# Gate/up of an encoder trunk: all engines in written order, evictions ahead of conversions, silu and products one product later

## The chip, the cores and the metric

The kernel runs on one core of a Trainium2 chip. The metric is the time of one execution in microseconds of device time (us). Before the change it is 2461.02 us, the median of 3 runs (2459.26 to 2463.18).

A core has five instruction streams that run beside each other and meet through semaphores: TensorE (PE in the profile, its weight loads PEld), VectorE (DVE), ScalarE (ACT), GpSimd (POOL) and SyncE (SP), which here issues the transfers between the chip's memory and the on-chip buffers. Matrix products land in eight banks of an accumulation memory (PSUM), from where VectorE or ScalarE has to take them. Each stream executes its instructions in the order in which the program holds them.

## The reference

Two layers of an encoder on 1024 tokens of width 1024. A layer has an attention half and a feed-forward half; the change touches the second, of which the core is

```
h = rms_norm(x, g_ffn[l]) * (1 + sc_f) + sh_f
gate, up = split_cols(h @ w_gu[l], (FFN_HIDDEN, FFN_HIDDEN))
x = x + gt_f * ((jax.nn.silu(gate) * up) @ w_down[l])
```

with `FFN_HIDDEN` = 2816. The vectors `sc_f`, `sh_f`, `gt_f` and three more for the attention half come from `mod = silu(c) @ w_mod[l] + b_mod[l]`, a product of one row with a 1024 x 6144 matrix per layer (the modulation).

## The kernel before

**Products in parts.** Each float32 operand is split into a high and a low part (`split_to`, line 205: ScalarE casts the high part, VectorE or GpSimd subtracts it from the source to get the low one), and `mm3` (line 197) multiplies in three matmuls. The matrix products of gate, up and down are done by a Strassen-Winograd scheme: a 2 x 2 block product in seven products instead of eight, with sums before and after. `PRODUCTS` (line 213) names the seven for gate/up in their order: number, the operand block of `h` it uses, and a bank a, b or c. Products 1, 6, 7 and 4 accumulate in bank a; between them a copy is taken out of the bank. So TensorE may not start product 6 before the copy after product 1 is taken, nor 7 before the copy "12" after 6, nor 3 (bank c) before the copy "22" after 5, nor 4 before the copy "x" after 7. One product is 4 x 3 = 12 matmuls of 128 x 128 by 128 x 512.

**Gate/up.** The 2816 columns of gate and of up are 11 pairs of column blocks. The loop runs over q = 0 to 21: even q is a gate block, odd q the up block of the same pair b = q // 2. For q below `EARLY` = 7 the first two products (1 and 2) are issued ahead of the loop, so the loop has five left for them and seven for the others. Operands on the weight side are made by a generator, `gu_parts` (line 1840): per q it loads the raw weights (`gu_raw`, names `wr`), makes four sums on VectorE (`ws`) and yields the converted parts (`wpt`). `ahead` holds up to 8 of them: `ahead.get()` (line 269) first fills the list to 8 and then takes one, and `ahead.fill()` after each product adds the next. The raw weights of odd q lie in buffers that before held blocks 2 and 3 of the activations (`x_tile`), and come free when their last split is done.

**After a product** (`gu_product`, line 1849): `take` copies a bank out on ScalarE, `add` adds a bank to an earlier copy on VectorE, `done` applies silu (ScalarE) for gate, or multiplies by up (GpSimd or VectorE). The result of a pair is two tiles `sg`, e and o, each of two halves. Two sets of these tiles take turns, so pair b + 2 overwrites pair b. They, too, lie in buffers of the activations.

**Down's operands** (`g_steps`, line 1900): a pair's four result blocks are stored (`gpd<-sg`), combined on VectorE by four subtractions (`sg<-sg`), and the combinations are stored as well. This is a list of 13 steps, of which one runs behind each product of the following pair (`g_step`); the stores come in steps 3, 9, 11 and 12, the subtractions in 8, 9 and 10. `gu_start` (line 1929) finishes what is left of the older pair when a new pair starts.

**Modulation** (`mod_stream`, line 353): in layer 0, from q = 7 on, each product is followed by one step of the next layer's modulation: a load of 128 x 512 weights (`wmt`) and one multiply-add on VectorE (`acc`), with two load buffers. In layer 1 nothing is left of it.

**The opening.** Ahead of the loop, `t2_part`, `t3_part` and `t4_part` (lines 1948 to 1976) make the remaining blocks of `h`: sums on VectorE in place (`xb`), then the splits `ht3`, `h22` and `ht4`, of which VectorE's halves are `ht3l`, `h22l` and `ht4l`.

**What sets the order.** Instructions are given to a scheduler, which may move them within an engine as long as data and buffers allow. `pin` (line 92) switches that off for chosen engines: each instruction is then bound to the one before it. In this loop, SyncE is pinned from the start (line 2003), ScalarE from the last q on (line 2008). Everything else is ordered by the scheduler.

Of the kernel before, what the change touches and what calls it, by code (L numbers as in the profile page):

```python
# [13 lines left out]
AF = mybir.ActivationFunctionType  # L14
ALU = mybir.AluOpType
# [8 lines left out]
H = 512  # L24
# [61 lines left out]
def trunk(ctx: ExitStack, tc, A, C, out):  # L86
# [266 lines left out]
    def mod_stream(psp, shared, until):  # L353


        pl, tag, bufs, width = shared
        acc = None
        while todo and todo[0] < until:
            l, g = todo[0]
            first = going["step"]  # L360
            if first == 0:
                going["acc"] = cp.tile([P, 1024], F32, name="acc", tag="acc")
            acc = going["acc"]
            halves = [(k, c0) for k in range(first, KC) for c0 in range(0, 1024, width)]
            loads = {}

            def load(i):
                k, c0 = halves[i]
                st = loads[i] = pl.tile([P, width], F32, name="wmt", tag=tag, bufs=bufs)
                g0 = g * 1024 + c0  # L370
                sp.dma_start(st, A["w_mod"][l, k * P : (k + 1) * P, g0 : g0 + width])

            if halves:
                load(0)
                yield
            for i, (k, c0) in enumerate(halves):
                if i + 1 < len(halves):
                    load(i + 1)
                mod_add(k, acc[:, c0 : c0 + width], loads.pop(i))
                yield  # L380
            going["step"] = KC
            mod_parts(slice(0, width), shared)
            while going["step"]:
                yield
                yield
                yield
                mod_flush(psp)
            yield
# [422 lines left out]
    for l in range(2):  # L811
# [1033 lines left out]
                raws = after or gu_raw(1)  # L1845

        sg, quads = {}, {}

        def gu_product(q, p, a):
            num, b, bank = p  # L1850
# [18 lines left out]
            def done(dst, src, eng=dve):  # L1869
                if up:  # L1870
                    eng.tensor_tensor(out=dst, in0=dst, in1=src, op=ALU.mult)
                else:
                    act.activation(dst, src, AF.Silu)

            if num == 1:
                take("11")
            elif num == 2:
                add("11")
                if e is not None:
                    done(e[:, lo], t["11"], pool)  # L1880
            elif num == 6:
                take("12", None if up else e[:, hi])
            elif num == 5:
                take("22", None if up else o[:, hi])
            elif num == 7:
                take("x")
                t22 = t["22"]
                pool.tensor_tensor(out=t22, in0=t22, in1=t["x"], op=ALU.add)
                done(o[:, hi], t["22"], pool)
            elif num == 3:  # L1890
                add("12")
                done(e[:, hi], t["12"], pool)
            else:
                done(o[:, lo], ps)
                if up:
                    steps.append(g_steps(q // 2, e, o))

        steps = []

        def g_steps(b, e, o):  # L1900


            b11, b12, b21, b22 = (t[:, i * H : (i + 1) * H] for t in (e, o) for i in range(2))

# [12 lines left out]

        def g_step():
            if steps:
# [80 lines left out]
        for part in (t3_part, t4_part):  # L2000
            for q in range(1, 4):
                part(q, *bs[q])
        pin([sp], True)
        for q in range(NF):
            if q % 2 == 0:
                gu_start(q // 2)
            if q == NF - 1:
                pin([act], True)
            if q < EARLY:
                up = q % 2  # L2010
                e = sg[q // 2][0][:, 0:H]
                if up:
                    pool.tensor_tensor(out=e, in0=e, in1=quads[q]["11"], op=ALU.mult)
# [339 lines left out]
```

## Time and profile before

| | |
|---|---|
| median of 3 runs | 2461.02 us (2459.26 to 2463.18) |
| the profiled execution | 2460.37 us, its span 2458.6 us |
| granted TensorE clock, mean | 0.991 |
| TensorE busy | 2390.3 us, 97% of the span |
| VectorE busy | 1821.8 us, 74% |
| ScalarE busy | 1224.9 us, 50% |
| GpSimd busy | 764.3 us, 31% |
| loop of gate/up, layer 0 | about 640 to 1044 us |
| loop of gate/up, layer 1 | about 1843 to 2227 us |

The span reaches from the first instruction to the last one. "PE ps_w" in the profile is a matmul of gate/up, "ps_d" one of down, "wpt" a converted part of a weight, "sg" a result tile, "u" a copy that was taken out of a bank, "gpd" the stored operands of down, "acc" the modulation's sum. All helpers record through line 49, so groups and rows are told apart by the tile names. A row of a timeline has start, duration, engine, line, operation, output and inputs, the count if several of a kind follow each other, and in brackets the idle time just before and what ended it.

### The profile page before, as it was taken

Reading aid. Unit: us, or ns where it says so; the run is one execution under the profiler, and the core shown is the slowest. Engines: PE = TensorE matmul, PEld = TensorE weight load, DVE = VectorE, ACT = ScalarE, POOL = GpSimd, SP = SyncE. Lnnn points to the kernel's source line nnn. Section 1 sums busy time; section 2 is a strip of 40 time slices with the busy share of each in tenths; the row PEclk is TensorE's granted clock in tenths of the full one; section 3 lists DMA queues with packets and bytes.
Section 4 is the critical chain, followed back from the end, with each engine's and each line's share of the span. In section 5 each row is a group of like instructions: output and inputs, shape, how many; then the busy total and the mean of one; then the engine's idle time right before and its main releaser. Section 6 shows DMA issues by size and latency. Waiting matters only on the chain.

```text
span 2458.6 us, 34285 instructions
## 1 busy us (share of the span) xinstructions
PE 2390.3 (97%) x12005; PEld 1992.7 (81%) x12005; DVE 1821.8 (74%) x2966; ACT 1224.9 (50%) x2306; POOL 764.3 (31%) x769
## 2 busy tenths in 40 slices
PE   8999999999999999999999999999999999999998
PEld 5787899878788877788887789987887888888886
DVE  5757999877967878587677679999698555446865
ACT  3422888954543333344544148888454333333443
POOL 1520444620244444300036114465005434430001
PEclk9999999999999999999999999999999999999999
DMA  8468205245345454496433851151624332229743
GB/s 287 147 177 287 54 14 146 57 151 167 95 142 173 158 168 140 154 287 201 129 116 106 259 195 27 41 152 44 210 90 141 125 115 95 99 102 283 215 134 110
DMA packets 285206, 356.04 MB, mean 145 GB/s; under 512 B 32997, under 2 KB 201533, under 8 KB 285033
## 3 DMA queue, kind: packets, MB, share of 16 engines
q1 hardware_dynamic: 277816, 341.12, 44.6%
q10 hardware_dynamic: 6912, 12.59, 1.6%
q8 instruction: 95, 1.56, 0.3%
q14 instruction: 79, 0.64, 0.1%
q0 software_dynamic: 304, 0.14, 0.0%
HBM read 269.62 MB, written 86.69 MB: 145 GB/s over the span
## 4 chain that ended last, share of the span: by engine, by line
PE 71%; DVE 11%; DMA 6%; issue 5%; ACT 4%; POOL 2%; SPq 1%; ACTq 0%; POOLq 0%; DVEq 0%
PE ps_w L49 30%; PE ps_d L49 10%; PE ps_o L49 7%; PE pv L49 6%; PE ps_ab L49 5%; PE T L49 4%; PE sC L49 3%; DVE wpt L49 2%; DMA wmt<-in_w_mod_dram 2%; PE ps_c L49 1%; ACT pr L49 1%; DMA zt<-skA 1%; PE sA L49 1%; DMA zAd<-zt 1%; DMA w<-in_w_down_dram 1%
## 5 line engine op out<-in xcount | busy, mean ns | idle before, releaser
L49 PE MATMUL ps_d<-wpt 128*128 128x512 f32 x1848 | 425.3, 390 | 2.0 <-DVE wpt L49 0.7
L49 PEld LDWEIGHTS ps_d<-wpt 128*128 128x128 f32 x1848 | 345.4, 188 | 77.2 <-DVE wpt L49 3.1
L49 POOL TENSOR_SCALAR pr<-pr,rs 128x1024 f32<-128x1024 f32 (+4 forms) x252 | 207.6, 826 | 308.5 <-DVE rs L49 290.7
L49 POOL TENSOR_TENSOR sg<-sg,u 128x512 f32<-128x512 f32 x86 | 124.2, 1445 | 360.9 <-ACT sg L49 228.0
L49 PE MATMUL pv<-pt,vs 128*128 128x256 f32 x1216 | 202.5, 297 | 8.0 <-DVE rs L49 2.3
L49 DVE TENSOR_TENSOR pt<-T,pt 128x512 fp32r<-128x512 f32 x304 | 199.4, 680 | 11.4 <-ACT pt L49 9.9
L49 ACT CAST pt<-T 128x512 fp32r<-128x512 f32 x304 | 170.2, 586 | 44.5 <-PE T L49 42.8
L49 PE MATMUL T<-identr,pr 128*128 128x128 f32 x1288 | 187.6, 273 | 2.2 <-ACT rb L49 1.0
L49 ACT COPY u<-ps_w 128x512 f32<-128x512 f32 x128 | 75.2, 587 | 215.1 <-PE ps_w L49 215.1
L49 PEld LDWEIGHTS pv<-pt,vs 128*128 128x128 f32 x1216 | 161.7, 190 | 23.2 <-DVE y L49 7.6
L49 DVE SCALAR_TENSOR_TENSOR acc<-wmt,condT,acc 128x512 f32<-128x512 f32 (+1 forms) x98 | 115.0, 1183 | 84.5 <-DMA wmt<-in_w_mod_dram 84.2
L49 DVE TENSOR_TENSOR wpt<-w,wpt 128x512 fp32r<-128x512 f32 x154 | 111.2, 722 | 84.0 <-ACT wpt L49 83.9
L49 PEld LDWEIGHTS T<-identr,pr 128*128 128x128 f32 x1288 | 153.1, 141 | 21.9 <-issue 3.2
L49 POOL TENSOR_TENSOR wpt<-ws,wpt 128x512 fp32r<-128x512 f32 x80 | 112.3, 1405 | 181.5 <-ACT wpt L49 139.3
L49 ACT CAST wpt<-w 128x512 fp32r<-128x512 f32 x154 | 95.5, 620 | 134.2 <-PE ps_d L49 127.9
L49 ACT CAST wpt<-ws 128x512 fp32r<-128x512 f32 x176 | 107.8, 622 | 56.4 <-issue 22.4
L49 ACT CAST wpt<-graw 128x512 fp32r<-128x512 f32 x154 | 95.0, 617 | 74.6 <-DMA graw<-gpd 65.2
L49 DVE TENSOR_TENSOR wpt<-ws,wpt 128x512 fp32r<-128x512 f32 x96 | 85.1, 895 | 59.1 <-ACT wpt L49 59.0
L49 DVE TENSOR_REDUCE rs<-sC 128x1 f32<-128x1024 f32 x96 | 116.4, 1218 | 6.4 <-PE sC L49 5.9
L49 DVE TENSOR_TENSOR wpt<-graw,wpt 128x512 fp32r<-128x512 f32 x154 | 110.4, 717 | 10.5 <-ACT wpt L49 10.4
L49 PE MATMUL ps_w<-ht3h,wpt 128*128 128x512 f32 x352 | 111.8, 399 | 6.4 <-ACT sg L49 6.4
L49 DVE TENSOR_TENSOR ws<-wr 128x512 f32<-128x512 f32 x88 | 78.8, 898 | 51.7 <-POOL wpt L49 48.7
(287 smaller groups left out, 6027.3 us busy)
## 6 DMA issues: line engine op xcount, KB each, us to landing
wr<-in_w_gu_dram SPq DMA_DIRECT2D x92, 512.0 KB, 4.2
gpd<-sg SPq DMA_DIRECT2D x154, 256.0 KB, 4.4
graw<-gpd SPq DMA_DIRECT2D x76, 512.0 KB, 3.7
w<-in_w_down_dram SPq DMA_DIRECT2D x110, 256.0 KB, 5.2
wmt<-in_w_mod_dram SPq DMA_DIRECT2D x48, 512.0 KB, 5.9
qk<-qkd SPq DMA_DIRECT2D x44, 512.0 KB, 7.3
wst<-in_w_o_dram SPq DMA_DIRECT2D x32, 512.0 KB, 3.5
wmt<-in_w_mod_dram SPq DMA_DIRECT2D x64, 256.0 KB, 3.5
```

The costliest lines, as they stand in the source:

```text
L49: ins = op(*args, **kwargs)
```

## The change

It makes the loop of gate/up run in written order on all five engines and changes what that order is.

- `pin` holds SyncE, TensorE, ScalarE, VectorE and GpSimd from the loop's start; TensorE, VectorE and GpSimd are let go after its last product.
- Within a product the order is: the matmuls, the copy or addition that empties the bank, the conversion of the part eight places ahead, then the silu or multiplication that the *preceding* product left (`done_later` puts it on the list `put_off`, `finish_later` runs it), then the step for down, then the modulation. Products 2, 5/7 and 3 are put off; product 4's own silu or multiplication is not.
- For the blocks with q below 7, whose product 2 lies ahead of the loop, a table `first_due` says behind which product the silu or multiplication of that result comes. For q = 1 it is done by VectorE instead of GpSimd.
- Down's steps for a pair start one product later, and the list has 14 entries: subtractions in 9, 10 and 11, stores in 3, 10, 12 and 13. `gu_start` finishes all of them (`g_finish(0)`). Pairs 0 and 1 are both started at q = 0.
- The modulation loads two halves before its first sum, and issues load i + 2 behind sum i instead of load i + 1 ahead of it. The number of buffers stays two.

```diff
             if halves:
                 load(0)
+                load(1)
                 yield
             for i, (k, c0) in enumerate(halves):
-                if i + 1 < len(halves):
-                    load(i + 1)
                 mod_add(k, acc[:, c0 : c0 + width], loads.pop(i))
+                if i + 2 < len(halves):
+                    load(i + 2)
                 yield
...
+            def done_later(*a):
+                put_off.append(lambda: done(*a))
+
             if num == 1:
                 take("11")
             elif num == 2:
                 add("11")
                 if e is not None:
-                    done(e[:, lo], t["11"], pool)
+                    done_later(e[:, lo], t["11"], pool)
...
-                done(o[:, hi], t["22"], pool)
+                done_later(o[:, hi], t["22"], pool)
             elif num == 3:
                 add("12")
-                done(e[:, hi], t["12"], pool)
+                done_later(e[:, hi], t["12"], pool)
             else:
                 done(o[:, lo], ps)
-                if up:
-                    steps.append(g_steps(q // 2, e, o))
+
+        def finish_later(n):
+            while len(put_off) > n:
+                put_off.pop(0)()
...
                 3: lambda: [put(*a) for a in (("11", b11), ("22", b22), ("21", b21))],
-                8: lambda: sub(b11, b12, b11),
-                9: lambda: (sub(b12, b22, b12), sub(b22, b22, b11), put("t1", b11)),
-                10: lambda: sub(b21, b21, b22),
-                11: lambda: (put("t3", b12), put("t2", b22)),
-                12: lambda: put("t4", b21),
+                9: lambda: sub(b11, b12, b11),
+                10: lambda: (sub(b12, b22, b12), sub(b22, b22, b11), put("t1", b11)),
+                11: lambda: sub(b21, b21, b22),
+                12: lambda: (put("t3", b12), put("t2", b22)),
+                13: lambda: put("t4", b21),
             }
-            return [due.get(i, lambda: None) for i in range(13)]
+            return [due.get(i, lambda: None) for i in range(14)]
...
         def gu_start(b):
-            g_finish(1)
+            g_finish(0)
...
-        pin([sp], True)
+        pin((sp, pe, act, dve, pool), True)
+        def early_first(q):
+
+            e = sg[q // 2][0][:, 0:H]
+            if q % 2:
+                eng = dve if q == 1 else pool
+                eng.tensor_tensor(out=e, in0=e, in1=quads[q]["11"], op=ALU.mult)
+            else:
+                act.activation(e, quads[q]["11"], AF.Silu)
+
+        first_due = {(0, 1): (0,), (0, 4): (1,), (1, 0): (2, 3), (4, 1): (4,), (4, 4): (5,), (6, 1): (6,)}
         for q in range(NF):
-            if q % 2 == 0:
+            if q % 2 == 0 and q != 2:
                 gu_start(q // 2)
...
+            if q == 0:
+                gu_start(1)
+            up = q % 2
             for i, p in enumerate(PRODUCTS[2 if q < EARLY else 0 :]):
+                n = len(put_off)
                 gu_product(q, p, ahead.get())
-                if i == 1 and q < EARLY and not up:
-                    act.activation(e, quads[q]["11"], AF.Silu)
+                new = len(put_off) - n
                 ahead.fill()
+                for early_q in first_due.get((q, i), ()):
+                    early_first(early_q)
+                finish_later(new)
+                if p[0] == 4 and up:
+                    put_off.append(lambda b=q // 2: steps.append(g_steps(b, *sg[b])))
                 g_step()
                 if q >= EARLY:
                     next(mods_due, None)
+        finish_later(0)
+        pin((pe, dve, pool), False)
```

What this does to the order of the instructions shows at three places. First, ScalarE at the opening of the loop, where TensorE waits for the copies `sg<-ps_w` and `u<-ps_w` of q = 0 (`ht3h`, `ht4h`: splits of activations; `wpt<-ws`: conversions of the weight sums for q = 1). Before:

```order
L49 CAST ht3h<-xb 128x512 x3
L49 COPY sg<-ps_w 128x512
L49 ACT_TABLE_LOAD
L49 ACTIVATE sg<-u 128x512
L49 CAST ht4h<-xb 128x512 x2
L49 ACTIVATE sg<-u 128x512
L49 COPY u<-ps_w 128x512
L49 COPY sg<-ps_w 128x512
L49 CAST ht4h<-xb 128x512
L49 ACTIVATE sg<-sg 128x512
```

and with the change:

```order
L49 CAST ht3h<-xb 128x512 x3
L49 CAST ht4h<-xb 128x512 x3
L49 CAST wpt<-ws 128x512 x3
L49 COPY sg<-ps_w 128x512
L49 CAST wpt<-ws 128x512
L49 COPY sg<-ps_w 128x512
L49 CAST wpt<-wr 128x512
L49 ACT_TABLE_LOAD
L49 ACTIVATE sg<-u 128x512
L49 COPY u<-ps_w 128x512
```

All three `ht4h` casts and three conversions stand ahead of the first copy now; the silus moved behind the second one.

Second, VectorE at the end of q = 3, where the four subtractions `sg<-sg` of pair 0 belong (`u<-u,ps_w` and `sg<-sg,ps_w` are the addition after product 3 and the multiplication after product 4 of q = 3). Before:

```order
L49 TENSOR_TENSOR sg<-sg 128x512
L49 TENSOR_TENSOR ws<-wr 128x512
L49 TENSOR_TENSOR sg<-sg 128x512
L49 TENSOR_TENSOR ws<-ws,wr 128x512
L49 TENSOR_TENSOR sg<-sg 128x512 x2
L49 TENSOR_TENSOR wpt<-ws,wpt 128x512
L49 TENSOR_TENSOR ws<-wr 128x512
L49 TENSOR_TENSOR ws<-wr,ws 128x512
L49 TENSOR_TENSOR wpt<-ws,wpt 128x512
L49 TENSOR_TENSOR u<-u,ps_w 128x512
```

and with the change:

```order
L49 TENSOR_TENSOR u<-u,ps_w 128x512
L49 TENSOR_TENSOR sg<-sg,ps_w 128x512
L49 TENSOR_TENSOR ws<-wr 128x512
L49 TENSOR_TENSOR wpt<-ws,wpt 128x512
L49 TENSOR_TENSOR sg<-sg 128x512 x4
L49 TENSOR_TENSOR ws<-wr,ws 128x512
L49 TENSOR_TENSOR wpt<-wr,wpt 128x512
```

The four subtractions moved from ahead of q = 3's last two results to behind them, into the start of q = 4.

Third, ScalarE in the last gate block (the same in every block from q = 8 on), where the silu `sg<-u` of product 2 stands. Before:

```order
L49 CAST wpt<-wr 128x512
L49 CAST wpt<-ws 128x512
L49 ACTIVATE sg<-u 128x512
L49 COPY sg<-ps_w 128x512
L49 CAST wpt<-ws 128x512
L49 COPY sg<-ps_w 128x512
```

and with the change:

```order
L49 CAST wpt<-wr 128x512
L49 CAST wpt<-ws 128x512
L49 COPY sg<-ps_w 128x512
L49 CAST wpt<-ws 128x512
L49 ACTIVATE sg<-u 128x512
L49 COPY sg<-ps_w 128x512
```

The silu moved behind the copy after product 6 and behind one more conversion.

More of the change, by code (lines that the diff above doesn't have):

```diff
@@ L1847, in trunk @@
         sg, quads = {}, {}
+        put_off = []
         def gu_product(q, p, a):
@@ L2002, in trunk @@
                 part(q, *bs[q])
-        pin([sp], True)
+        pin((sp, pe, act, dve, pool), True)
[7 more added lines that the diff above has]
+        first_due = {(0, 1): (0,), (0, 4): (1,), (1, 0): (2, 3), (4, 1): (4,), (4, 4): (5,), (6, 1): (6,)}
         for q in range(NF):
-            if q % 2 == 0:
+            if q % 2 == 0 and q != 2:
                 gu_start(q // 2)
[L2007 to L2013, printed above, removed]
+            if q == 0:
+                gu_start(1)
+            up = q % 2
             for i, p in enumerate(PRODUCTS[2 if q < EARLY else 0 :]):
+                n = len(put_off)
                 gu_product(q, p, ahead.get())
-                if i == 1 and q < EARLY and not up:
-                    act.activation(e, quads[q]["11"], AF.Silu)
+                new = len(put_off) - n
                 ahead.fill()
+                for early_q in first_due.get((q, i), ()):
[3 more added lines that the diff above has]
+                    put_off.append(lambda b=q // 2: steps.append(g_steps(b, *sg[b])))
                 g_step()
```

## The prediction

> **What bounds the kernel now.** I read the page's chain of work first, then the two gate/up stages in windows, then the timelines of the engines at TensorE's gaps.
>
> ```profile
> span 2458.6 us, 34285 instructions
> PE 71%; DVE 11%; DMA 6%; issue 5%; ACT 4%; POOL 2%; SPq 1%; ACTq 0%; POOLq 0%; DVEq 0%
> 652.05:1113.80 461.75, 452.89 (x1960) 371.43 (x1960) 342.89 (x441) 176.30 (x314) 172.31 (x118) 0.99 0.55 173
> 1854.74:2296.95 442.21, 441.69 (x1944) 364.49 (x1944) 260.55 (x340) 177.58 (x314) 162.93 (x118) 1.00 0.45 143
> ```
>
> The chain that ends last is TensorE for 71% of the span. The two windows cover the same work in layer 0 and layer 1, from one matmul of gate/up to one matmul of down; after the length come the busy times of PE, PEld, DVE, ACT and POOL. In layer 1 TensorE is busy 441.69 of 442.21 us, so nothing in this stretch can be gained there. Layer 0 takes 461.75, 19.54 more. It issues 16 more matmuls (those of the modulation); at 442.21 / 1944 = 0.227 us each they are 3.6 us. The other **15.9 us** are stalls, and they are all that the change can win here.
>
> The stalls have one form. The rows of the timeline give start, duration, engine, and in brackets the idle time before and what ended it:
>
> ```profile
> 808.78 0.73 PE L49 MATMUL ps_w<-ht3h,wpt 128*128 128x512 f32 x2 [0.63 <-ACT sg L49]
> 862.81 1.13 PE L49 MATMUL ps_w<-ht2h,wpt 128*128 128x512 f32 x2 [1.96 <-ACT u L49]
> 930.83 0.91 PE L49 MATMUL ps_w<-ht3h,wpt 128*128 128x512 f32 x2 [2.57 <-ACT sg L49]
> 1013.75 1.22 PE L49 MATMUL ps_w<-ht3h,wpt 128*128 128x512 f32 x2 [3.22 <-ACT sg L49]
> ...
> 929.67 0.63 ACT L49 ACTIVATE sg<-u 128x512 f32<-128x512 f32 x1 [6.15 <-DVE u L49]
> 930.21 0.57 ACT L49 COPY sg<-ps_w 128x512 f32<-128x512 f32 x1
> ...
> DVE acc L49 <- DMA wmt<-in_w_mod_dram: 45.7, 27, 5.4
> ```
>
> Before the third stall, ScalarE stands 6.15 us at a silu whose input VectorE has not added yet; the copy that empties TensorE's bank is queued behind it. VectorE is late because it waits for modulation weights, 45.7 us in 27 waits over this stage. TensorE waits 0.63 + 1.96 + 2.57 + 3.22 = 8.4 us; most of the rest is a lower clock afterwards:
>
> ```profile
> 860.00:880.00 20.00, 18.04 (x72) 14.41 (x71) 12.16 (x17) 7.71 (x14) 9.86 (x7) 0.91 0.32 106
> 1000.00:1020.00 20.00, 16.78 (x62) 13.23 (x61) 14.16 (x21) 5.03 (x10) 3.84 (x4) 0.83 0.13 40
> ```
>
> The granted clock falls to 0.91 and 0.83 of these 20 us, so one stall costs a further 1.8 to 3.4 us. I take 2.6 us for a stall of 2 us or more.
>
> **Part 1: copies before silus (gain).** A silu or product now stands behind the next product's copy and conversion, about one product (12 x 0.227 = 2.7 us) later, and the late silu at 929.67 would have held nothing up. All four stalls have this cause: at most 15.9 us come back. VectorE is now fixed too, so work that its free order did before a modulation sum now waits behind it. The second modulation load is issued ahead, but has still only two buffers: it cannot start before the sum two places earlier. I take **13 us** of gain, with 0 and 15.9 as ends. The same four silus, copies and conversions are executed; no work is added or removed anywhere.
>
> **Part 2: the opening of the loop (loss, both layers).** These are the rows of the opening in layer 0; layer 1 has the same ones 1202.7 us later.
>
> ```profile
> 645.88 0.61 PE L49 MATMUL ps_w<-ht3h,wpt 128*128 128x512 f32 x2
> 649.49 0.73 PE L49 MATMUL ps_w<-ht4h,wpt 128*128 128x512 f32 x2 [0.73 <-ACT u L49]
> 652.05 0.73 PE L49 MATMUL ps_w<-h22h,wpt 128*128 128x512 f32 x2 [1.60 <-ACT sg L49]
> ...
> 644.83 0.59 ACT L49 COPY sg<-ps_w 128x512 f32<-128x512 f32 x1 [0.70 <-DVE ht3l L49]
> 655.71 2.18 ACT L49 CAST wpt<-ws 128x512 fp32r<-128x512 f32 x4 [1.25 <-DVE ws L49]
> ...
> 645.26 0.74 DVE L49 SCALAR_TENSOR_TENSOR xb<-xb,vecs,t 128x512 f32<-128x512 f32 x1
> 647.92 3.46 DVE L49 TENSOR_TENSOR ht4l<-xb,ht4h 128x512 fp32r<-128x512 f32 x2
> 654.99 0.69 DVE L49 TENSOR_TENSOR ws<-ws,wr 128x512 f32<-128x512 f32 x1
> 655.60 0.68 DVE L49 TENSOR_TENSOR sg<-sg,ps_w 128x512 f32<-128x512 f32 x1
> ...
> 647.45 3.38 POOL L49 TENSOR_TENSOR sg<-sg,u 128x512 f32<-128x512 f32 x2 [112.73 <-ACT sg L49]
> ...
> L49 SPq DMA_DIRECT2D wr<-in_w_gu_dram x92: 367/383/1117, 616.0 to 2207.0; - x92
> DMA to landing us min/median/max: 3.4/4.2/5.8
> ```
>
> Now the first copy (take 12 of product 6) runs at 644.83 and TensorE starts product 7 (ht3h) at 645.88 without waiting. In the new ScalarE order three `ht4h` casts and three `wpt<-ws` conversions stand ahead of that copy, because the loop's first `ahead.get()` fills the list before the product is issued, and ScalarE is held to that order. When are they done? VectorE is as before until the row at 645.26. Then, at 0.6 us from start to start (654.99 to 655.60), come two sums and a split, the first `ht4l` (done near 647.9), a split, the second `ht4l`, a sum, and the last `ht4l`, which waits for its cast and ends near 651.2. GpSimd no longer runs beside them, under which the two `ht4l` took 3.46. The first `ht4l` frees the buffer of gate/up's next raw weights; those land 3.4 us (the least of the row) later with nothing ahead of them, at 651.5. From there: two sums 1.3 us; two casts and the VectorE halves 2.0; the third sum 0.6; its cast 0.6 after a hand-over; the copy 0.6. That is 5.2, so product 7 starts near 656.7, **10.8 us** after it does now. The two waits of the old opening, 0.73 + 1.60 and 0.6 around them, 2.9 us, vanish in it. With 2.6 us of lower clock: 10.8 - 2.9 + 2.6 = **10.5 us per layer**. Ends: 10.4 us idle and 1.8 of clock (9.3), or a landing after 5.8 us and 3.4 of clock (13.7). Whether TensorE makes this up is answered by the window of layer 1 above: it is busy to the end, so it does not.
>
> **Part 3: down's sums beside the reuse of `sg` (loss, both layers).** The first two pairs have five products per column block in the loop, ten per pair, while the list of down's steps now has 14 entries, starts one product later, and is finished at once when a new pair starts. So steps 10 to 13, with one sum of step 9 just before them, all come at the start of q = 4 and again of q = 6, where the new pair takes the tile over. The new program shows the four `sg<-sg` together behind `sg<-sg,ps_w`, which cannot run before product 4 of the block before is done.
>
> ```profile
> 698.02 0.61 PE L49 MATMUL ps_w<-ht2h,wpt 128*128 128x512 f32 x2
> 703.46 0.61 PE L49 MATMUL ps_w<-ht3h,wpt 128*128 128x512 f32 x2
> ...
> 701.10 0.67 DVE L49 TENSOR_TENSOR sg<-sg,ps_w 128x512 f32<-128x512 f32 x1
> 712.83 2.38 DVE L49 TENSOR_TENSOR sg<-sg 128x512 f32<-128x512 f32 x2
> ...
> L49 SPq DMA_DIRECT2D gpd<-sg x154: 319/434/1462, 680.5 to 2242.7; - x154
> DMA to landing us min/median/max: 2.0/4.4/5.8
> ```
>
> q = 4 starts at 698.02 (call it 0), and its third product at 703.46, 5.4 us later; take 12 must be done by then. VectorE: the multiplication, the next sum and a conversion with its cast to 3.3 us, two of the four sums to 4.6 (some of it slowed by GpSimd, as the pair at 712.83 was: 2.38 instead of 1.3). SyncE then stores the second sum; it lands 4.0 us later, at 8.7, between the row's 2.0 and 4.4 since fewer transfers share the queue than in a burst of seven. The copy takes 0.6 and TensorE goes on at 9.4: **4.0 us** late. At q = 6 one more sum stands ahead: **4.6**. With 2.6 of clock each, 6.6 + 7.2 = **13.8 us per layer**. Ends: a landing in 2.0, no slowing and no loss of clock give 1.5 + 2.1 = 3.6; slowed sums, a landing in 5.8 and 3.4 of clock give about 11 each, 22.
>
> [...]
>
> **What moves at no cost.** The end of gate/up into down keeps its order on ScalarE and TensorE; VectorE's four last sums come after its addition instead of before it, still well before TensorE's last products end, and down's first weights keep their cover. If that cover were gone, a weight's landing time would show at the first matmul of `ps_d`.
>
> **The sum.** 2 x (10.5 + 13.8) - 13 = +35.6 us. The profiled execution took 2460.37 us (span 2458.6 and 1.8 around it), 0.65 under the median 2461.02. 2460.4 + 35.6 = **2496 us**.
>
> **Rivals.** (a) *The stores are in time*: they land near their least time and the sums run unslowed, so that part 3 costs next to nothing: 2460.4 + 21 - 13 = 2468. For it speaks the 2.0 us minimum; against it, that sums and store follow each other in 5.4 us. (b) *VectorE becomes the bound in layer 0*: fixed in order, its 45.7 us of waits for modulation weights delay sums and conversions, and nothing of the 13 us comes: 2509. Against it: 342.89 of 461.75 us busy leaves slack. (c) *Faster*: copies ahead of silus return 15.9 us and the opening's own 2 x 2.9, at most 2438.7. This needs the three conversions at the opening done before the first copy is wanted, near 645; it decides when parts 2 and 3 together cost under 8 us per layer. The opening alone has 9.3 as its lower end, and the program order itself shows the conversions ahead of the copy. I price this rival at 2447, half of the opening's waits left. (d) *Nothing comes of it*: opening at its lower end, no store late, the full gain: 2460.4 + 18.6 - 15.9 = 2463.
>
> **How the numbers follow.** Forecast 0.60, (a) 0.15, (b) 0.12, (c) 0.08, (d) 0.05. All losses at their ends together would give 2471 to 2532; these seldom fall together, so with the rivals the range is 2464 to 2518. A measurement of this kernel can tell about 0.2%, 4.9 us, from no change. Faster by more: (c), 0.08. Within: (d) and a third of (a), 0.10. Slower: 0.82.
>
> **What would show it.** Right: in the new profile TensorE idle some 11 us near 646 to 657 and 1849 to 1860, ended by ScalarE's `sg`, with `wpt<-ws` casts ahead of that copy; two idle times of 3 to 5 us some 57 and 91 us after that, ended by a copy that waited for `gpd<-sg`; no wait for `sg` behind a silu between 805 and 1020; more clock slices at half. Wrong: the first copy still near 645; the stores landing before 6 us from a block's start; new gaps from q = 7 on in layer 1.

## The result and the profile after

The change makes the kernel slower: **2502.11 us** (median of 4 runs, 2501.25 to 2503.92) against 2460.14 us for the kernel before (4 runs). The ratio is 1.0178 with a 95% interval of 1.0165 to 1.0191. The forecast was 2496 us. The profiled execution took 2502.04 us.

The page of the kernel after: no engine does more work than before, TensorE is only spread over more time.

```profile
span 2500.2 us, 34298 instructions
PE 2398.8 (96%) x12005; PEld 1999.9 (80%) x12005; DVE 1815.6 (73%) x2968; ACT 1224.0 (49%) x2306; POOL 764.3 (31%) x767
```

The view that groups instructions shows at once where the time went. The columns are count, then busy time and mean ns of one, then the idle time of the engine just ahead of the group and who ended it. First before, then after, for the matmuls of product 7 (`ht3h`), which must wait until the copy "12" of product 6 is out of the bank:

```profile
L49 PE MATMUL ps_w<-ht3h,wpt 128*128 128x512 f32 x352 | 111.8, 399 | 6.4 <-ACT sg L49 6.4
```

```profile
L49 PE MATMUL ps_w<-ht3h,wpt 128*128 128x512 f32 x352 | 119.7, 424 | 43.9 <-ACT sg L49 43.9
```

The idle time ahead of this one product rises from 6.4 to 43.9 us, all of it ended by ScalarE's copy into `sg`. The mean matmul becomes 25 ns slower, which is the lower clock behind the gaps: in the trace after, 47 of the 352 start while the granted clock is 0.50 and take 625 ns in the mean, the others 393; before, 13 start so. The other operands of gate/up lose no time any more: `ht2h`, `h22h` and `ht4h` had 2.0, 3.2 and 1.5 us of such idle time before and have 0.0 now.

The next view cuts out the loop of gate/up in windows, from its first matmul to the same matmul in down, layer 0 and then layer 1 (length, busy times of PE, PEld, DVE, ACT and POOL with their counts, clock, DMA share, GB/s). Before, then after:

```profile
640.44:1113.80 473.36, 462.18 (x2000) 378.48 (x1998) 354.50 (x456) 182.85 (x325) 175.69 (x120) 0.99 0.54 171
1843.14:2296.95 453.81, 450.98 (x1984) 371.54 (x1982) 272.15 (x355) 184.13 (x325) 166.31 (x120) 1.00 0.45 141
```

```profile
640.32:1134.43 494.11, 465.87 (x2000) 381.22 (x1998) 357.31 (x458) 181.80 (x325) 172.99 (x119) 0.97 0.52 164
1866.03:2338.07 472.04, 454.97 (x1984) 375.34 (x1982) 265.89 (x358) 183.19 (x325) 169.46 (x119) 0.98 0.43 136
```

The two stretches are 20.7 and 18.2 us longer, together 39.0 of the 42 us. Below, the delay of a matmul is how much later it starts than the same matmul in the kernel before, counted from the first matmul of its loop. The experiments below are compared by these two stretches, since equal instructions ahead of the loop differ by some us between runs (see the end).

TensorE's timeline gives the places. These are the rows of the loop of the kernel after with more than 1 us of idle time ahead of them (in brackets) ended by `sg`, all of layer 0 and the last of layer 1's three, which are 1225.7 us later than those of the opening, q = 4 and q = 6 in layer 0:

```profile
656.89 1.22 PE L49 MATMUL ps_w<-ht3h,wpt 128*128 128x512 f32 x2 [10.97 <-ACT sg L49]
716.21 1.22 PE L49 MATMUL ps_w<-ht3h,wpt 128*128 128x512 f32 x2 [2.60 <-ACT sg L49]
748.45 0.73 PE L49 MATMUL ps_w<-ht3h,wpt 128*128 128x512 f32 x2 [3.35 <-ACT sg L49]
790.44 0.85 PE L49 MATMUL ps_w<-ht3h,wpt 128*128 128x512 f32 x2 [1.97 <-ACT sg L49]
872.49 0.96 PE L49 MATMUL ps_w<-ht3h,wpt 128*128 128x512 f32 x2 [2.97 <-ACT sg L49]
955.13 1.22 PE L49 MATMUL ps_w<-ht3h,wpt 128*128 128x512 f32 x2 [3.56 <-ACT sg L49]
997.31 0.73 PE L49 MATMUL ps_w<-ht3h,wpt 128*128 128x512 f32 x2 [1.38 <-ACT sg L49]
...
1974.12 0.73 PE L49 MATMUL ps_w<-ht3h,wpt 128*128 128x512 f32 x2 [3.60 <-ACT sg L49]
```

There are three kinds of place, and each has its own cause; 790.44 belongs to the second kind.

**The opening** (656.89, and the same in layer 1). ScalarE's timeline:

```profile
649.78 0.62 ACT L49 CAST ht4h<-xb 128x512 fp32r<-128x512 f32 x1 [1.91 <-DVE xb L49]
653.08 1.14 ACT L49 CAST wpt<-ws 128x512 fp32r<-128x512 f32 x2 [2.68 <-DVE ws L49]
655.74 0.62 ACT L49 CAST wpt<-ws 128x512 fp32r<-128x512 f32 x1 [1.52 <-DVE ws L49]
656.26 0.58 ACT L49 COPY sg<-ps_w 128x512 f32<-128x512 f32 x1
```

The copy takes 0.58 us, and its data has been ready for 13 us: product 6 ended at 643.2. What takes the time is the queue: the last `ht4h` cast and three conversions, each idle until VectorE has made its source.

**The blocks q = 4 and q = 6** (716.21, 748.45 and the same in layer 1). VectorE, SyncE and ScalarE around them:

```profile
711.95 2.86 DVE L49 TENSOR_TENSOR sg<-sg 128x512 f32<-128x512 f32 x4
712.66 2.50 SPq L49 DMA_DIRECT2D gpd<-sg  x4
715.57 0.59 ACT L49 COPY sg<-ps_w 128x512 f32<-128x512 f32 x1 [4.27 <-DVE ws L49]
...
744.21 2.86 DVE L49 TENSOR_TENSOR sg<-sg 128x512 f32<-128x512 f32 x4
744.92 3.98 SPq L49 DMA_DIRECT2D gpd<-sg  x7
747.81 0.59 ACT L49 COPY sg<-ps_w 128x512 f32<-128x512 f32 x1 [4.25 <-DMA gpd<-sg]
```

The four late subtractions, their stores and the copy that overwrites the tile follow each other as forecast. At q = 6 the bracket names the store; at q = 4 it names a sum on VectorE that ended within 0.2 us of the copy's start, but a copy into `sg` reads nothing of `ws`. Which of the two held it is one question for the experiments.

The same happens once more at q = 8 of layer 0, where the prediction had nothing. Pair 2 has 5 + 7 = 12 products for the 14 steps of its list, so its last three stores come only in q = 8, and there, too, the copy waits for a store:

```profile
785.11 1.46 SPq L49 DMA_DIRECT2D gpd<-sg  x3
789.81 0.59 ACT L49 COPY sg<-ps_w 128x512 f32<-128x512 f32 x1 [1.79 <-DMA gpd<-sg]
```

The delay grows by 3.9 us over q = 8 in layer 0; in layer 1 TensorE has no such wait there. No experiment tried this place alone.

**Layer 0 from q = 12 on** (872 to 997). The silu that stood ahead of the copy is gone from there, and yet the copy is late:

```profile
948.01 1.51 DVE L49 SCALAR_TENSOR_TENSOR acc<-wmt,condT,acc 128x512 f32<-128x512 f32 x1 [0.18 <-DMA wmt<-in_w_mod_dram]
951.19 0.75 DVE L49 SCALAR_TENSOR_TENSOR acc<-wmt,condT,acc 128x512 f32<-128x512 f32 x1 [1.67 <-DMA wmt<-in_w_mod_dram]
...
952.46 0.68 DVE L49 TENSOR_TENSOR ws<-wr 128x512 f32<-128x512 f32 x1
953.17 0.69 DVE L49 TENSOR_TENSOR ws<-ws,wr 128x512 f32<-128x512 f32 x1
...
953.98 0.62 ACT L49 CAST wpt<-ws 128x512 fp32r<-128x512 f32 x1 [9.36 <-DVE ws L49]
954.50 0.58 ACT L49 COPY sg<-ps_w 128x512 f32<-128x512 f32 x1
```

ScalarE stands 9.36 us at a conversion; the copy is the next instruction. The conversion's sum `ws` (953.17) stands on VectorE behind two modulation sums, of which the second waits for its weights. In the view of waits over 760 to 1070 us this is now the largest wait of ScalarE (us, times, longest):

```profile
ACT wpt L49 <- DVE ws L49: 132.2, 40, 9.4
```

### The profile page after: what moved, and what is told of

It is laid out like the page before. It is cut to its first block, busy times and chain, and to the rows that moved or that the text cites. A ratio compares the mean times of both kernels' runs of the same rounds, so it can differ in the third digit from the quotient of the medians.

```text
span 2500.2 us, 34298 instructions
## 1 busy us (share of the span) xinstructions
PE 2398.8 (96%) x12005; PEld 1999.9 (80%) x12005; DVE 1815.6 (73%) x2968; ACT 1224.0 (49%) x2306; POOL 764.3 (31%) x767
## 4 chain that ended last, share of the span: by engine, by line
PE 72%; DVE 10%; DMA 6%; issue 5%; ACT 4%; POOL 3%; SPq 0%; ACTq 0%; POOLq 0%; DVEq 0%
PE ps_w L49 28%; PE ps_d L49 14%; PE ps_o L49 6%; PE pv L49 6%; PE ps_ab L49 5%; PE T L49 4%; PE sC L49 3%; DMA wmt<-in_w_mod_dram 2%; PE ps_c L49 1%; ACT pr L49 1%; DMA gpd<-sg 1%; DMA zt<-skA 1%; PE sA L49 1%; DMA zAd<-zt 1%; DVE ws L49 1%
## 5 line engine op out<-in xcount | busy, mean ns | idle before, releaser
L49 POOL TENSOR_TENSOR sg<-sg,u 128x512 f32<-128x512 f32 x84 | 129.6, 1550 | 353.4 <-ACT u L49 323.1
L49 PE MATMUL ps_w<-ht3h,wpt 128*128 128x512 f32 x352 | 119.7, 424 | 43.9 <-ACT sg L49 43.9
L49 DVE TENSOR_TENSOR wpt<-ws,wpt 128x512 fp32r<-128x512 f32 x96 | 77.2, 809 | 111.9 <-ACT wpt L49 111.9
L49 PEld LDWEIGHTS ps_w<-ht3h,wpt 128*128 128x128 f32 x352 | 72.1, 208 | 63.5 <-ACT sg L49 48.1
```

The costliest lines, as they stand in the source:

```text
L49: ins = op(*args, **kwargs)
```

## The experiments

The theory from these traces: three separate faults, each a single instruction that the fixed order puts in front of the copy TensorE waits for; a conversion on ScalarE at the opening, the late store at q = 4 and q = 6, and in layer 0 a sum on VectorE behind the modulation. The main rival: a fixed order as such is what costs, so that a mended stall comes back at a later product. All experiments start from the changed kernel except the last one. The table gives what they took, and how much longer or shorter than in the kernel before the two stretches of the windows above are.

| experiment | time, us | layer 0 | layer 1 |
|---|---|---|---|
| the change | 2502.11 | +20.7 | +18.2 |
| 1 slow filling at the opening | 2488.70 | +18.2 | +12.9 |
| 2 down's steps in a list of 10 | 2475.07 | +9.3 | +9.6 |
| 3 copies of q = 4 and 6 elsewhere | 2479.77 | +10.8 | +9.6 |
| 4 VectorE free | 2469.32 | +1.9 | +7.2 |
| 5 ScalarE free | 2487.20 | +14.0 | +12.8 |
| 6 sums one product earlier | 2474.26 | +0.3 | +14.0 |
| 7 edits of 2 and 6 | 2465.14 | -4.4 | +8.8 |
| 8 edits of 1, 2 and 6 | 2446.01 | -12.8 | -1.3 |
| 9 edits of 1 and 2, VectorE free | 2454.09 | -6.3 | -1.4 |
| 10 only SyncE fixed | 2449.30 | -10.0 | -0.8 |
| 11 the modulation's loads alone | 2455.66 | -4.0 | -0.3 |

Where nothing else is said a time is that of one run, beside runs of the kernel before of 2457.79 to 2460.59 us (medians).

**1. Slow filling at the opening.** The list of converted parts is brought to 8 only by the end of the first block, so that the first copy has no conversion ahead of it.

```diff
-                gu_product(q, p, ahead.get())
+                ahead.fill(1)
+                gu_product(q, p, ahead.have.pop(0))
                 new = len(put_off) - n
-                ahead.fill()
+                ahead.fill((4, 3, 4, 5, 7)[i] if q == 0 else 8)
```

> The changed kernel (2502 us), with the list of converted parts filled slowly in the first block, so that no conversion stands ahead of the first two copies. Theory (the conversions ahead of the first copy hold TensorE up, 10.3 us in layer 0 and 10.2 in layer 1): product 7 of q = 0 starts near 646 again instead of 657, the opening costs less than in the kernel before (at most 2.9 us), about 2478 to 2483 us. Rival (TensorE would wait there anyway, for the raw weights that land at 651.5): the idle time only moves to a later product of q = 0 or 1, and the time stays within 5 us of 2502.

Measured: 2488.70 us, above the theory's range. The stall of 10.97 us is gone, but two others stand in its place:

```profile
644.72 0.73 PE L49 MATMUL ps_w<-h22h,wpt 128*128 128x512 f32 x2 [1.17 <-ACT sg L49]
660.37 1.22 PE L49 MATMUL ps_w<-ht3h,wpt 128*128 128x512 f32 x2 [4.22 <-ACT u L49]
```

So the conversions ahead of the copy were the cause of the opening's stall, and by this edit about half of its price moves on to q = 1 (at the first matmul of q = 4 the delay is still 4.5 us in layer 0 and 5.7 in layer 1, after 10.1 and 9.9): the three parts filled behind the last product of q = 0 stand ahead of the first copy of q = 1. The rival is half right here.

**2. Down's steps of pairs 0 and 1 in a list of 10**, which ends before the pair's tile is taken over; the subtractions come in steps 6 to 8, the stores in 3 and 7 to 9.

```diff
+            if b < 2:
+                due = {
+                    3: due[3],
+                    6: due[9],
+                    7: due[10],
+                    8: lambda: (sub(b21, b21, b22), put("t3", b12), put("t2", b22)),
+                    9: due[13],
+                }
+                return [due.get(i, lambda: None) for i in range(10)]
             return [due.get(i, lambda: None) for i in range(14)]
```

> The changed kernel, with the steps for down of the first two pairs brought forward to 3, 6, 7, 8 and 9, so that none is left when their tiles are reused at q = 4 and q = 6. Theory (late subtractions and the landing of their stores hold up the copy, 4.0 + 4.8 us in layer 0 and 3.9 + 5.3 in layer 1 with the lower clock): both gaps go in both layers, 18 us less, about 2484. Rival (the copy is late because VectorE's other work of that place is late): the gaps stay at 2 us or more, time above 2495.

Measured: 2475.07 us, 9 us below what the theory had. The stalls at q = 4 and q = 6 are gone in both layers and come back nowhere; the stretches lose 11.5 and 8.6 us against the change, and 5.8 us more lie ahead of layer 0's loop (see the end).

**3. The copies of q = 4 and q = 6 go elsewhere.** The late subtractions and stores stay as they are; only what they hold up is changed.

```diff
-                take("12", None if up else e[:, hi])
+                take("12", None if up or q in (4, 6) else e[:, hi])
...
-                take("22", None if up else o[:, hi])
+                take("22", None if up or q in (4, 6) else o[:, hi])
```

> The changed kernel, in which the two copies after products 6 and 5 of q = 4 and q = 6 go to spare copies u instead of straight into the result tile sg; the order inside the loop stays, and the four late subtractions and stores stay where they are. Theory S (part 3 of the prediction: the copy waits because it overwrites a block whose late store has not landed): the idle times of 2.6 and 3.4 us at q = 4 and q = 6 fall below 1 us in both layers, 14 to 18 us come back: 2484 to 2489 us. Theory W (the copy is late because it stands behind a conversion whose sum VectorE makes after the four subtractions, whatever tile the copy goes to): the idle times stay at 2 to 3.5 us: 2496 us or more.

Measured: 2479.77 us, below the range of theory S; the stalls are gone. ScalarE and TensorE at q = 4:

```profile
708.64 0.58 ACT L49 COPY u<-ps_w 128x512 f32<-128x512 f32 x1
712.92 0.62 ACT L49 CAST wpt<-ws 128x512 fp32r<-128x512 f32 x1 [3.71 <-DVE ws L49]
...
714.08 0.74 PE L49 MATMUL ps_w<-h22h,wpt 128*128 128x512 f32 x2 [0.32 <-ACT u L49]
```

The copy now runs at 708.64, 4.3 us ahead of the conversion behind it, which still waits for `ws`. So in the changed kernel it was held by the tile that it overwrites; the bracket that named `ws` gave the event nearest in time, not the cause. The stretches lose 10.0 and 8.7 us, nearly as in experiment 2: this is the price of part 3. Some 4 us more of the gain lie outside the two stretches, 2.6 of them ahead of layer 0's loop (see the end).

**4. VectorE free**: ordered by the scheduler, the other four engines fixed.

```diff
-        pin((sp, pe, act, dve, pool), True)
+        pin((sp, pe, act, pool), True)
```

> The changed kernel with VectorE alone left to the scheduler, the other four engines as in the change. Theory A (in layer 0 from q = 8 on, ScalarE's conversion waits for a sum that stands on VectorE behind modulation sums, because VectorE's order is fixed): the gaps from q = 8 on mostly go, and the subtractions at q = 4 and 6 are moved forward too, so only the opening's 10 us per layer are left: 2460 + 20.5 less up to 15.9, 2465 to 2480. Rival B (it is the modulation loads that hold VectorE up in any order, as in the kernel before): gaps in layer 0 of the old size, 15 us together, 2480 or more.

Measured: 2469.32 us. The opening keeps 9.2 us of idle time, q = 4 and q = 6 have none, and layer 0's products from q = 7 on gain 5.5 us against the kernel before. One stall of 2.84 us stays there, at 869.36, behind a silu whose input VectorE made late.

**5. ScalarE free**, the other four fixed.

```diff
-        pin((sp, pe, act, dve, pool), True)
+        pin((sp, pe, dve, pool), True)
```

> The changed kernel with ScalarE alone ordered by the scheduler; SyncE, TensorE, VectorE and GpSimd stay fixed. Theory A1 (the opening and the stalls from q = 7 on come from ScalarE's fixed order, where a conversion stands in front of the copy; only the stalls at q = 4 and q = 6 come from VectorE's): the 11 us at the opening shrink below 4 us, the stalls at q = 4 and q = 6 stay at 2 to 4 us each: 2465 to 2485 us. Theory A2 (VectorE's fixed order is the cause everywhere from q = 4 on, and ScalarE's only at the opening): as A1 in the opening, but the stalls at q = 8 to 20 of layer 0 stay too: 2480 to 2492 us.

Measured: 2487.20 us, as theory A2 has it. At the opening no idle time above 1.22 us is left. The stalls at q = 4 (3.58 us), q = 6 (4.94 us) and in layer 0 stay, because the scheduler, too, puts a conversion ahead of the copy. In layer 0:

```profile
941.59 0.75 DVE L49 SCALAR_TENSOR_TENSOR acc<-wmt,condT,acc 128x512 f32<-128x512 f32 x1 [1.45 <-DMA wmt<-in_w_mod_dram]
...
942.85 0.68 DVE L49 TENSOR_TENSOR ws<-wr 128x512 f32<-128x512 f32 x1
943.57 0.69 DVE L49 TENSOR_TENSOR ws<-ws,wr 128x512 f32<-128x512 f32 x1
...
944.37 0.62 ACT L49 CAST wpt<-ws 128x512 fp32r<-128x512 f32 x1 [0.78 <-DVE ws L49]
944.90 0.58 ACT L49 COPY sg<-ps_w 128x512 f32<-128x512 f32 x1
```

Experiments 4 and 5 divide the loss: the opening belongs to ScalarE's fixed order, nearly all the rest to VectorE's.

**6. Sums one product earlier.** Each sum of the weights is put one product ahead of its conversion, and so ahead of a modulation sum; the order stays fixed.

```diff
-            yield part(a12)
+            ready = part(a12)
         s1, s2, s3, s4 = sums()
         dve.tensor_tensor(out=s1, in0=a21, in1=a22, op=ALU.add)
         sub(s2, s1, a11)
-        yield part(s2)
-        yield part(s1)
+        if first:
+            yield ready
+        ready = part(s2)
         sub(s3, a11, a21)
-        yield part(s3)
+        yield ready
+        ready = part(s1)
         sub(s4, a12, s2)
+        yield ready
+        yield part(s3)
         yield part(s4)
```

> The changed kernel with each weight sum computed one product ahead of its conversion. Theory A: the conversions ahead of the copies no longer wait for VectorE, the gaps at 869, 951 and 995 us go (3.1 + 3.7 + 1.5 us and the lower clock behind them, 10 to 13 us together), the one at 788, which waits for a store, stays: 2489 to 2492. Rival B: VectorE is as late as before since it waits for the modulation's loads, the gaps stay: 2500 to 2504.

Measured: 2474.26 us, 15 us below the theory's range, which counted only the three stalls that the change had made. These are gone; at q = 8 one of 1.17 us is left, which still waits for a store. ScalarE's wait for the sums, over the same stretch of layer 0, shrinks from 132.2 us in 40 waits:

```profile
ACT wpt L49 <- DVE ws L49: 33.5, 11, 4.6
```

From the first matmul of q = 7 in layer 0 to the end of the stretch the delay moves by -15.0 us, where the change has +1.1. So nearly all of the 15.9 us comes that the prediction had as the most the modulation's stalls could give. (The edit also gains 3.5 us in layer 0 and 3.6 in layer 1 at q = 4 and q = 6.)

**7 and 8. The edits together.** Experiment 7 has the list of 10 and the earlier sums; experiment 8 has the slow filling as well, spread over two blocks instead of one:

```diff
+                ahead.fill(1)
+                gu_product(q, p, ahead.have.pop(0))
                 new = len(put_off) - n
-                ahead.fill()
+                ahead.fill(((4, 3, 4, 5, 5), (6, 6, 7, 7, 8))[q][i] if q < 2 else 8)
```

> The same without the edit of the opening: steps of pairs 0 and 1 in a list of 10, each sum one product ahead of its conversion. Theory A: the opening stays at about 10 us of idle time in each layer, nothing else is lost, and layer 0's modulation part gains about 14 us: 2460.4 + 2 x 9.5 - 14 = about 2465 us (2459 to 2470), 10 to 20 us above the run with all three edits. Rival B (the edits don't add): 2474 us or more, as with either of them alone.

> Three edits together on the changed kernel: at the opening the list of parts is filled slowly (one level per product, reaching 8 only at the end of q = 1), the steps of pairs 0 and 1 stand in a list of 10, and each sum of a product's weights is computed one product ahead of its conversion. Theory A (the three losses are separate faults of where the fixed order puts single instructions): the opening costs 0 to 5 us per layer instead of 10, the stalls at q = 4 and q = 6 are gone, and layer 0's modulation part keeps its gain of about 14 us, so that the kernel is faster than before: 2440 to 2457 us, most likely 2450. Rival B (a fixed order as such costs, and a stall that is mended comes back at a later product): 2462 us or more.

Measured: 2465.14 us for 7, and 2446.01 us for 8 (median of 6 runs, 2442.98 to 2448.30), where the kernel before took 2460.00 (median of 11): ratio 0.9945, interval 0.9929 to 0.9962. The rival falls: the effects add, and nothing comes back later. With all three edits TensorE hardly waits in either layer:

```profile
637.93:1098.53 460.60, 455.76 (x1999) 374.28 (x1998) 357.31 (x459) 182.59 (x324) 177.23 (x119) 1.00 0.55 176
1830.94:2283.46 452.52, 450.52 (x1983) 371.61 (x1982) 260.47 (x357) 182.90 (x324) 165.17 (x119) 1.00 0.45 142
```

Between 7 and 8 only the opening differs: 8.4 and 10.1 us per layer. Against the kernel before, experiment 8 gains nearly all of its time in layer 0 from q = 7 on, 12.6 us, where that kernel had its four stalls; which part of the change takes them away was not separated.

**9. Edits of 1 and 2 with VectorE free**, the slow filling as in experiment 8.

> The slow filling at the opening and the list of 10 steps for pairs 0 and 1, with VectorE ordered by the scheduler and the other four engines fixed; the sums stand where the change has them. Theory A: the opening costs 0 to 5 us per layer, no stall at q = 4 and q = 6, and the layer 0 modulation part gains about 5 us, as with VectorE free alone: 2453 to 2464 us. Rival B (the losses are those of the fixed ScalarE order, which is still there): 2469 us or more, no better than with VectorE free alone.

Measured: 2454.09 us, within the range. Stalls of 1.40 and 1.98 us stay in layer 0 that experiment 8 doesn't have.

**10. Only SyncE fixed**, as before the change; all other parts of the change stay.

```diff
-        pin((sp, pe, act, dve, pool), True)
+        pin([sp], True)
```

> The changed program, with only SyncE's order fixed in the loop, as before the change: the put-off silus and multiplications, the later steps and the modulation's early load stay, but TensorE, ScalarE, VectorE and GpSimd are ordered by the scheduler. Theory A (the fixed order places conversions and sums in front of what TensorE waits for): the idle 11 us at the opening and the stalls at q = 4 and q = 6 are gone or below 1.5 us each, and the time lies within 2450 to 2468 us. Rival C (what is put off is itself too late, whoever orders it): stalls of 2 to 4 us stay at q = 4 and q = 6, and the time is 2480 us or more.

> The kernel with only SyncE's order fixed again, timed in rounds: if the other parts of the change gain by themselves, its ratio to before lies at 0.993 to 0.998 with an interval below 1; if the single time was luck of the stages ahead of the loop, where equal programs differ by some us, the interval holds 1.

Measured: 2449.30 us in one run, just below theory A's range; timed again 2448.44 us (median of 5), ratio 0.9958, interval 0.9943 to 0.9972. Without the fixed order the rest of the change is a small gain, and the fixed order costs some 54 us on top of it (2502.11 - 2448.44). In the group shown first:

```profile
L49 PE MATMUL ps_w<-ht3h,wpt 128*128 128x512 f32 x352 | 108.9, 391 | 3.4 <-ACT sg L49 3.4
```

In layer 0's loop the scheduler's order on ScalarE is, as far as the tile names tell, that of the kernel before except for one silu that comes earlier: putting the silus off has been undone by it, so the gain isn't theirs. VectorE's order differs in many places.

**11. The modulation's loads alone**, in the kernel before:

```diff
             if halves:
                 load(0)
+                load(1)
                 yield
             for i, (k, c0) in enumerate(halves):
-                if i + 1 < len(halves):
-                    load(i + 1)
                 mod_add(k, acc[:, c0 : c0 + width], loads.pop(i))
+                if i + 2 < len(halves):
+                    load(i + 2)
                 yield
```

> The kernel before with one part of the change alone: the modulation loads two halves ahead and issues load i + 2 behind sum i. Theory A (what is left of the change without the fixed order gains in layer 0's modulation, by these loads): 5 to 9 us faster than before inside layer 0's loop and nothing in layer 1: 2450 to 2457 us. Rival C (the gain comes from the silus and multiplications that are put off, or from the multiplication of q = 1 on VectorE): no change by more than 2 us, 2458 to 2463 us.

Measured: 2455.66 us (median of 10), ratio 0.9999, interval 0.9990 to 1.0008. The theory behind it falls: these loads alone give nothing that a measurement can tell, though the profiled run has 4.0 us less in layer 0's loop. Where the 10 us of experiment 10 come from is therefore open; down's later steps and the multiplication of q = 1 on VectorE are left, and weren't tried alone.

## Why the prediction was right in sign and where its terms were off

**The bound and the opening (part 2): right.** TensorE bounds both stretches, and what it loses it doesn't make up. Product 7 was forecast to start at 656.7 and started at 656.89; the delay at the first matmul of q = 4 is 10.1 us in layer 0 and 9.9 in layer 1, against a term of 10.5. Experiments 1, 5 and 8 show the cause: without conversions ahead of the copy the stall is gone.

**Down's sums (part 3): right mechanism, term too large, one place missed.** Forecast 13.8 us per layer. From the first matmul of q = 4 to that of q = 7 the kernel before takes 40.80 us and the kernel after 50.39 and 50.48, so 9.6 and 9.7 us were lost; experiment 3 gives 10.0 and 8.7. Two numbers were off. The step "it lands 4.0 us later" is the first: the second subtraction ended near 713.4, and the copy started at 715.57, so the store landed within 2.2 us, near the row's minimum of 2.0. The step "With 2.6 of clock each" is the second: the idle times of 2.60 and 3.35 us made delays of 4.3 and 5.3, so the clock cost 1.7 and 2.0 us. Of the two idle times only the second lies within the "3 to 5 us" that were to show it. The late store at q = 8 in layer 0, 3.9 us, the prediction didn't have at all.

**The modulation's stalls (part 1): wrong, and the largest error.** Forecast 13 us of gain; from the first matmul of q = 7 to the end of the stretch the delay grew by 1.1 us, and without the 3.9 of q = 8 it would have shrunk by only 2.8. The four old stalls are gone as forecast, since no silu stands ahead of a copy. The step that failed is that the copy would then be held up by nothing. One conversion still stands ahead of it, as the order quoted with the change shows, and its sum now stands on VectorE behind a late modulation sum. With VectorE's order free these stalls are gone (experiment 4). The prediction named that risk ("work that its free order did before a modulation sum now waits behind it") and allowed too little for it, 2.9 of the 15.9 us. Experiment 6 shows it: with the sums ahead of the modulation 15.0 of the 15.9 us come.

**The rivals.** Rival (b), nothing of part 1 comes, is what happened, though not by VectorE being the bound: it is busy 357 of 494 us in this stretch. With (b)'s 2509 and part 3 at its measured 19.3 us instead of 27.6 one gets 2509 - 8.3 = 2501. Rivals (a), (c) and (d) are out: the stores landed near their least time, as (a) has it, but were late all the same in both layers, and the first copy came at 656.26.

**The sum.** Part 1 was 14.0 us too good, part 3 8.3 us too bad and the opening 1.0 too bad. Not forecast were 1.4 us of gain behind layer 1's loop and 2.7 us of loss outside the two stretches. 14.0 - 8.3 - 1.0 - 1.4 + 2.7 = 6.0 us, the difference between forecast and result. The forecast was near by luck: two large errors had opposite signs.

## What to carry to other kernels

Fixing the order of an engine makes every instruction ahead of a bank's copy a possible wait (here up to 10.97 us, at the opening), so for each copy that the bounding engine needs, follow what stands ahead of it back through all engines, to the load or sum that is made last. Removing one late instruction from in front of a copy gains only if the next one in the queue is on time: here a conversion stood next, and ScalarE waited up to 9.36 us at it. When prefetched work shares a queue with such copies, fill the prefetch list slowly at the start of a loop (8.4 and 10.1 us per layer between experiments 7 and 8), and make sums a step before the conversions that use them (in experiment 6 layer 0 gains 15.0 us from q = 7 on).

## What the hardware showed beside this

**What TensorE's idle time did to the granted clock.** In the traces before and after, the granted clock is 1.00 or 0.50, and all its changes inside the span lie whole multiples of 3.413 us apart. Cut into pieces of 3.41 us along these changes, such pieces in a row (PE's busy time is the second number, the clock the third from the end) are, first in the kernel after around the stall of 2.60 us, then in experiment 1 around one of 3.61 us (q = 6, layer 1):

```profile
712.40:715.81 3.41, 1.21 (x6) 0.67 (x4) 2.90 (x5) 0.24 (x1) 0.00 (x0) 1.00 0.66 244
715.82:719.22 3.40, 3.01 (x7) 2.43 (x8) 1.05 (x2) 2.49 (x5) 1.27 (x1) 0.50 0.68 216
...
1957.17:1960.57 3.40, 1.47 (x7) 0.89 (x5) 3.05 (x5) 0.22 (x1) 0.00 (x0) 1.00 0.28 106
1960.58:1963.98 3.40, 1.73 (x7) 1.42 (x8) 0.91 (x2) 2.03 (x4) 1.18 (x1) 1.00 1.01 370
1963.99:1967.39 3.40, 3.40 (x16) 2.81 (x15) 1.29 (x2) 1.81 (x4) 1.49 (x3) 1.00 0.69 218
```

The first stall leaves 2.20 us idle in one piece (3.41 - 1.21), and the next piece is at 0.50, which costs an estimated 1.7 us of work, half of 3.41. The second, longer stall is split 1.93 to 1.67, and the piece behind each part is at 1.00. In the two stretches of the traces before and after, cut in this way, 527 pieces at 1.00 had 0 to 1.62 us idle and were each followed by one at 1.00; 12 had 1.92 us or more and were each followed by one at 0.50. One of the 12 is at q = 8 of the kernel after, 787.49 to 790.90, with 1.97 us. So in these traces the length of a stall alone doesn't tell whether the clock falls behind it: the stall of 2.60 us lost clock, and that of 3.61 us, spread over two pieces, did not.

**The stage before moves by some us between runs.** Ahead of the loop the instructions of the change and of the first three experiments stand in the same order, yet layer 0's loop starts at 640.32 us in the change, 635.23 in experiment 1 and 634.48 in experiment 2. Most of this arises between 185 and 205 us, where the DMA engines are busy throughout (share 1.01 to 1.03): TensorE gets 65 matmuls done there in the change and 85 in experiment 2; the 20 of difference, at 19.24 / 85 = 0.226 us each, are an estimated 4.5 us of the 5.8 between these two.

```profile
185.00:205.00 20.00, 16.66 (x65) 12.96 (x65) 15.41 (x18) 2.92 (x5) 2.41 (x3) 0.91 1.01 328
```

```profile
185.00:205.00 20.00, 19.24 (x85) 15.61 (x84) 15.15 (x18) 3.67 (x5) 2.42 (x3) 1.00 1.03 358
```

Why one run gets through this stretch faster than another was not looked into. For a change inside one stage the stage's own windows are therefore a sharper measure than the whole time of a single run.
